# Output projection of a hybrid block: four of eight blocks of the contraction by seven half-size products

## The chip, the cores and the metric

The kernel runs on one core of a Trainium2 chip. A core has five engines that work side by side, each through its own instructions in order: TensorE (PE) multiplies matrices into PSUM, VectorE (DVE) and ScalarE (ACT) work elementwise, GpSimd (POOL) does small work and issues DMAs, and SyncE (SP) issues DMAs. They wait for each other on semaphores. The metric is the time of one execution on the device in microseconds (us); the times here are medians over several runs.

## The reference

One layer on x of 512 rows (tokens) by 1024 columns in fp32: a SwiGLU feed-forward half step, a mixer of dilated window attention and mLSTM, and a second feed-forward half step. What the change touches is the end of the mixer and the norm behind it:

```
merged = jax.nn.sigmoid(g_a) * (att @ w_att_branch) + jax.nn.sigmoid(g_m) * (ml @ w_mlstm_branch)
y = merged @ w_out                       # (512 x 1024) @ (1024 x 1024)
x = x + rmsnorm(y, mix_post_g)
f = swiglu(rmsnorm(x, ffn2_pre_g), ffn2_w_gate, ffn2_w_up, ffn2_w_down)
x = x + 0.5 * rmsnorm(f, ffn2_post_g)
```

All is computed to about fp32 precision. PE multiplies values of a shorter format (F32R), so that each operand is split in a high part, a rounded copy, and a low part, the rest, and each product is three: high by high, low by high, high by low.

## The kernel before

The kernel is one long program in stages: feed-forward 1, projections, attention, mLSTM, merge, output projection, feed-forward 2. It works on the 512 tokens as four tiles of 128 (index t), and keeps the activations of a product transposed, with the contracted dimension on the 128 partitions in 8 blocks (index dt or kk).

**Merge.** A loop over dt = 0 to 7 (`for dt in range(KD)`) makes block dt of the merged rows, transposed, 128 x 512: two products on PE, a few operations on DVE and ACT on `t1`, then ACT writes the high part meTh[:, dt] and DVE the low part meTl[:, dt]. The gates of block dt + 2 (tiles qa_gm, qb_gm) are computed in between.

**Output projection.** `down` goes over the eight blocks kk. `load_w` loads w_out's block of 128 x 1024 by a DMA from SP into a staging buffer wf (a ring of three), casts it on ACT to wh and computes the low part wl on DVE, five buffers each. `step` issues three 128x512 matmuls into one PSUM bank acc_o, for four token tiles and two column halves b: eight banks, all of PSUM. The first four blocks are multiplied block by block (kk < n - KEEP, with KEEP = 4). The last four are held and multiplied bank by bank, so that a token tile gets finished early.

**Norm behind it.** When tile t is complete, `PostNorm.bank` squares each bank on ACT (jk_pmx), sums on DVE (v_pmx), takes the power on POOL (r_pmx), and DVE multiplies by the gain (fg_mx) and adds to x. `prenorm` makes the next normed rows h_f of the tile in the same way (jk_f, v_f, r_f). Then PE transposes h_f into pt_f (`turn_norm`, eight transposes), ACT copies hTh_f from it and DVE computes hTl_f. The `todo` list issues these transposes between the matmuls of later banks, and the first products pg_b of feed-forward 2 read hTh_f and hTl_f by halves of 256 tokens. Their first weights, bgu00 and on, go through the same staging ring and `load_w`.

**Order.** The program is written once in Python; a planner then sets each engine's order by the costs and ready times that it assumes, keeping to the data's dependences. `Order` and `issue_after` pin a chain of instructions on an engine to the order in which they are written. The queues run strictly in that order on the chip.

The down products of both feed-forwards already work by seven products (class `Down`), and `down` already takes ready accumulators, with the second column half negated (flip).

Of the kernel before, what the change touches and what calls it, by code (L numbers as in the profile page):

```python
# [10 lines left out]
F32 = mybir.dt.float32  # L11
F32R = mybir.dt.float32r
BF16 = mybir.dt.bfloat16
AF = mybir.ActivationFunctionType
ALU = mybir.AluOpType

P = 128
T = 512
NT = T // P
D = 1024  # L20
KD = D // P
# [11 lines left out]
WMAX = 1024  # L33
# [6 lines left out]
def tile_hybrid_block(ctx: ExitStack, tc: tile.TileContext, a: dict):  # L40
    nc = tc.nc

    ids = ctx.enter_context(tc.tile_pool(name="ids", bufs=1))
    wpool = ctx.enter_context(tc.tile_pool(name="wpool", bufs=1))
    hpool = ctx.enter_context(tc.tile_pool(name="hpool", bufs=1))
    const = ctx.enter_context(tc.tile_pool(name="const", bufs=1, side="right"))
    act = ctx.enter_context(tc.tile_pool(name="act", bufs=1, side="right"))
# [10 lines left out]
    work = Work()  # L58
# [6 lines left out]
    def pair(name):  # L65
        return [bank(f"{name}_{b}") for b in range(2)]
# [22 lines left out]
    def load_w(src, name, n=1024, after=(), flip=False):  # L89
        wf = act.tile([P, WMAX], F32, tag="wf", bufs=3, name=f"wf_{name}")[:, :n]  # L90
        nc.sync.dma_start(wf, src)
        with ExitStack() as st:
            for i in after:
                st.enter_context(tc.issue_after(i))
            wh = wpool.tile([P, WMAX], F32R, tag="wh", bufs=5, name=f"wh_{name}")[:, :n]
            cast_w(wh, wf, flip)
            wl = wpool.tile([P, WMAX], F32R, tag="wl", bufs=5, name=f"wl_{name}")[:, :n]
            m = T if flip else n
            nc.vector.tensor_tensor(wl[:, :m], wf[:, :m], wh[:, :m].bitcast(F32), op=ALU.subtract)  # L99
            if flip:  # L100
                nc.vector.scalar_tensor_tensor(wl[:, T:], wf[:, T:], -1.0, wh[:, T:].bitcast(F32), op0=ALU.mult,
                                               op1=ALU.subtract)
        return wh, wl
# [146 lines left out]
    H = T // 2  # L250
    ADD, SUB, MUL = ALU.add, ALU.subtract, ALU.mult
# [410 lines left out]
    with new_pool("ffn_a") as fa:  # L662
# [99 lines left out]
        todo = []  # L762
# [596 lines left out]

    gctx = ExitStack()  # L1360
    mg = gctx.enter_context(tc.tile_pool(name="merge", bufs=1))
    meTh = mg.tile([P, KD, T], F32R, name="meTh")
    meTl = mg.tile([P, KD, T], F32R, name="meTl")
    class Tiles:
        def __init__(self, i):
            self.i = i
# [7 lines left out]
    for dt in range(KD):  # L1374
        if dt % 2 == 0:
            wA = load_w(a["wA"][dt // 2], f"wA{dt}")
        wM = load_w(a["wM"][dt], f"wM{dt}")
        p2 = pair(f"p2_{dt}")
        o = (dt % 2) * 512
        ws(p2[0], (wA[0][:, o:o + 512], wA[1][:, o:o + 512]), HEADS, atth, attl, (late, 6))  # L1380
        for _ in late:
            pass
        ws(p2[1], wM, KD, mlTh, mlTl)
        t1 = t1s[dt]
        for b in range(2):
            nc.vector.scalar_tensor_tensor(t1[:, b, :], t1[:, b, :], 1.0, p2[b], op0=ALU.add, op1=ALU.mult)
        nc.vector.tensor_tensor(t1[:, 0, :], t1[:, 0, :], t1[:, 1, :], op=ALU.add)
        nc.scalar.mul(meTh[:, dt, :], t1[:, 0, :], 0.5)
        nc.vector.scalar_tensor_tensor(meTl[:, dt, :], t1[:, 0, :], 0.5, meTh[:, dt, :].bitcast(F32),
                                       op0=ALU.mult, op1=ALU.subtract)  # L1390
        if dt + 2 < KD:
            late = branch_gates(dt + 2)
            next(late)
# [8 lines left out]
    def post2(t):  # L1402
        if t == 2:
            hT2.extend(new_hT("f2"))
        return PostNorm(t, g_mpost, [(work, "tmp"), (mm, "m0h")][t % 2], "mx")

    def finish2(t):
        h = prenorm(t, g_f2pre, [(work, "h"), (mm, "m0l")][t % 2], "f2")
        todo.append(lambda: turn_norm(t, h, *hT2, "f2"))

    pins = down(KD, lambda kk: a["wout"][kk], lambda kk: (meTh[:, kk, :], meTl[:, kk, :]), post2, finish2, todo, "o")
    gctx.close()
    mctx.close()

# [48 lines left out]
def _layout(inp):  # L1463
    f = lambda n: np.asarray(inp[n])[0]

    def cols(w):
        k, n = w.shape
        return w.reshape(k // P, P, n // P, P).transpose(2, 1, 0, 3).reshape(n // P, P, k)

    def rows(w):  # L1470
        k, n = w.shape
        return w.reshape(k // (2 * P), 2, P, n).transpose(0, 2, 1, 3).reshape(k // (2 * P), P, 2 * n)

    r = {"x": np.asarray(inp["x"])[0]}
    for i, n in ((1, "ffn1"), (2, "ffn2")):
        r[f"wgu{i}"] = np.concatenate([cols(f(f"{n}_w_gate")), cols(f(f"{n}_w_up"))], 2)
        wd = f(f"{n}_w_down").reshape(NF, P, D)
        r[f"wd{i}"] = wd
        wq = wd[:18].reshape(2, 9, P, 2, 512).transpose(0, 3, 2, 1, 4)
        r[f"wdq{i}"] = wq[:, :, :, :8].reshape(2, 2, P, 4, 1024).transpose(3, 0, 1, 2, 4)  # L1480
        r[f"wdh{i}"] = wq[:, :, :, 8]
        r[f"{n}_pre_g"], r[f"{n}_post_g"] = f(f"{n}_pre_g"), f(f"{n}_post_g")
    r["mix_pre_g"], r["mix_post_g"], r["mlstm_head_g"] = f("mix_pre_g"), f("mix_post_g"), f("mlstm_head_g")
    w = f("w_in")
    qa, ka, va = w[:, 0:1536], w[:, 1536:3072], w[:, 3072:4608]
    qkm, vm, om = w[:, 4608:6656], w[:, 6656:7680], w[:, 7680:8704]
    wi, wf_, ga, gm = w[:, 8704:8708], w[:, 8708:8712], w[:, 8712:9736], w[:, 9736:10760]
    place = np.arange(P)
    place[:64] = (place[:64] + 32) % 64

    def heads(w):
        w = w.reshape(D, 3, 4, P).copy()
        w[:, 1:] = w[:, 1:][..., place]
        return cols(w.reshape(D, 1536)).reshape(3, 4, P, D)

    q, k = heads(qa), heads(ka)
    r["wqk"] = np.stack([q, k], 2).transpose(1, 0, 2, 3, 4)
    v0g = [np.concatenate([va[:, h * 256:(h + 1) * 256], g], 1) for h, g in enumerate((wi, wf_))]
    r["wv0"] = np.stack([v.reshape(KD, P, 260).transpose(1, 0, 2).reshape(P, KD * 260) for v in v0g])

    v12 = [np.concatenate([va[:, 512 + h * P:512 + (h + 1) * P], va[:, 1024 + h * P:1024 + (h + 1) * P]], 1)
           for h in range(4)]
    r["wv12"] = np.stack([rows(np.concatenate(v12[2 * hp:2 * hp + 2], 1)) for hp in range(2)])
    r["gbias"] = np.stack([f("mlstm_i_bias"), f("mlstm_f_bias")], 1)
    qm, km = cols(qkm[:, 0:1024]), cols(qkm[:, 1024:2048])
    r["wmqk"] = np.stack([np.concatenate([qm[2 * h:2 * h + 2], km[2 * h:2 * h + 2]]) for h in range(4)])
    r["wvo"] = np.stack([rows(np.concatenate([vm[:, h * 256:(h + 1) * 256], om[:, h * 256:(h + 1) * 256]], 1))
                         for h in range(4)])
    r["wgm"] = np.stack([cols(ga), cols(gm)], 1)
    r["wA"] = cols(f("w_att_branch")).reshape(4, 2, P, 512).transpose(0, 2, 1, 3).reshape(4, P, 1024)  # L1510
    r["wM"] = cols(f("w_mlstm_branch"))
    r["wout"] = f("w_out").reshape(KD, P, D)
    cw = np.concatenate([f("conv_w"), f("conv_b")[None, :]], 0)
    r["convwb"] = cw.reshape(5, 16, P).transpose(2, 1, 0)
    return r
# [17 lines left out]
```

## Time and profile before

| What | Value |
|---|---|
| Median of 3 runs | 1333.09 us (1333.08 to 1333.26) |
| Profiled execution | 1333.12 us, its span 1331.2 us |
| Granted TensorE clock | 1.00 |
| PE busy | 1323.6 us, 99% |
| DVE, ACT, POOL busy | 1002.9, 640.4, 79.6 us |
| First and last matmul into acc_o start | 944.4 and 989.5 us |
| Matmuls into acc_o | 192, each 389 ns with overlap |

The page gives the busy time of each engine over the span. A matmul's busy time overlaps the next one's, so that the distance between two starts, not its length, says what it costs. "idle before" in brackets on a row is the time that an engine stood still, and the arrow names what ended it. The chain of waits goes back from the last instruction over whatever released each one. Times in windows and timelines are counted from the start of the span.

### The profile page before, as it was taken

What the parts mean: (1) busy time and instruction counts of PE and PEld (TensorE: products, weight loads), DVE (VectorE), ACT (ScalarE), POOL (GpSimd) and SP (SyncE); (2) the same over time, 40 slices, a digit from 0 to 9 for tenths busy, and PEclk for the clock granted to TensorE, in tenths of its full rate; (3) what the DMA queues carried; (4) which work ended last, traced back from release to release, by engine and by line L of the source; (5) the groups of instructions that cost most, each with busy time, mean ns of one, the idle gap of its engine ahead of it and who ended that gap; (6) DMA issues with size and microseconds to landing.
All of it is one profiled execution on the core that took longest, in us unless ns stands there. A gap on an engine that the chain in (4) does not pass through costs nothing.

```text
span 1331.2 us, 20808 instructions
## 1 busy us (share of the span) xinstructions
PE 1323.6 (99%) x8283; PEld 1197.0 (90%) x8283; DVE 1002.9 (75%) x1553; ACT 640.4 (48%) x1046; POOL 79.6 (6%) x118
## 2 busy tenths in 40 slices
PE   9999999999999999999999999999999999999998
PEld 9999999888998888888888889999889999999886
DVE  7999898798765556575756777776379999897886
ACT  6444444566634544544544444444265444445662
POOL 1000000230300000000000000000010000001220
PEclk9999999999999999999999999999999999999999
DMA  5333332896433422412222212335413333335972
GB/s 198 96 104 111 104 104 96 206 236 167 136 115 117 142 69 91 158 64 80 80 79 80 70 58 80 96 97 188 151 41 99 110 109 104 105 110 140 250 156 80
DMA packets 43906, 155.55 MB, mean 117 GB/s; under 512 B 4996, under 2 KB 5004, under 8 KB 43552
## 3 DMA queue, kind: packets, MB, share of 16 engines
q1 hardware_dynamic: 33120, 116.96, 26.6%
q0 software_dynamic: 10672, 37.25, 11.5%
q8 instruction: 65, 1.06, 0.3%
q14 instruction: 33, 0.27, 0.1%
q10 hardware_dynamic: 16, 0.00, 0.0%
HBM read 147.91 MB, written 6.29 MB: 116 GB/s over the span
## 4 chain that ended last, share of the span: by engine, by line
PE 99%; DVE 0%; DVEq 0%; POOLq 0%; ACT 0%; issue 0%; ACTq 0%
PE qb_b L338 10%; PE qb_a L338 10%; PE pq L189 8%; PE pm L189 7%; PE p L189 6%; PE qa_b L338 4%; PE qa_a L338 4%; PE qb_gm L1089 4%; PE acc_o L243 3%; PE accb_b L536 3%; PE accb_a L536 3%; PE pvo L1215 2%; PE pvo L1217 2%; PE pvo L1216 2%; PE accc_a L536 2%; PE accc_b L536 2%
## 5 line engine op out<-in xcount | busy, mean ns | idle before, releaser
L189 PE MATMUL pq<-hTh_mx,wh_qk 128*128 128x512 f32 x160 | 63.2, 395 | 0.0
L189 PE MATMUL pq<-hTl_mx,wh_qk 128*128 128x512 f32 x160 | 62.4, 390 | 0.0
L99 DVE TENSOR_TENSOR wl_qk<-wf_qk,wh_qk 128x1024 fp32r<-128x1024 f32 x24 | 29.4, 1223 | 31.1 <-ACT wh_qk L85 14.4
L189 PE MATMUL pm<-hTh_mx,wh_mqk 128*128 128x512 f32 x128 | 50.3, 393 | 0.0
L1215 PE MATMUL pvo<-wh_vo,hTh_mx 128*128 128x512 f32 x128 | 50.2, 392 | 0.0
L189 PE MATMUL pm<-hTl_mx,wh_mqk 128*128 128x512 f32 x128 | 49.9, 390 | 0.0
L1217 PE MATMUL pvo<-wl_vo,hTh_mx 128*128 128x512 f32 x128 | 49.9, 390 | 0.0
L1216 PE MATMUL pvo<-wh_vo,hTl_mx 128*128 128x512 f32 x128 | 49.8, 389 | 0.0
L99 DVE TENSOR_TENSOR wl_mqk<-wf_mqk,wh_mqk 128x1024 fp32r<-128x1024 f32 x16 | 19.6, 1224 | 35.7 <-ACT wh_mqk L85 26.7
L85 ACT CAST wh_qk<-wf_qk 128x1024 fp32r<-128x1024 f32 x24 | 25.0, 1046 | 40.6 <-issue 11.6
L189 PE MATMUL pq<-hTh_mx,wl_qk 128*128 128x512 f32 x160 | 39.6, 389 | 0.0
L263 ACT CAST wh_a<-cd_a 128x1024 fp32r<-128x1024 f32 x19 | 19.9, 1048 | 40.8 <-DVE cd_a L263 40.8
L263 ACT CAST wh_b<-cd_b 128x1024 fp32r<-128x1024 f32 x19 | 19.9, 1049 | 40.7 <-DVE cd_b L263 40.7
L338 PE MATMUL qa_b<-hTh_f,wh_b 128*128 128x256 f32 x152 | 38.2, 284 | 0.0
L338 PE MATMUL qa_a<-hTh_f,wh_a 128*128 128x256 f32 x152 | 38.2, 284 | 0.0
L338 PE MATMUL qa_b<-hTl_f,wh_b 128*128 128x256 f32 x152 | 38.1, 283 | 0.0
L338 PE MATMUL qa_a<-hTl_f,wh_a 128*128 128x256 f32 x152 | 38.1, 283 | 0.0
L85 ACT CAST wh_mqk<-wf_mqk 128x1024 fp32r<-128x1024 f32 x16 | 16.8, 1048 | 41.9 <-PE pvo L1216 22.9
L1010 DVE SCALAR_TENSOR_TENSOR z<-pm,cw,z 128x511 f32<-128x511 f32 (+2 forms) x48 | 35.3, 744 | 1.4 <-ACT z L1008 0.9
L189 PEld LDWEIGHTS pq<-hTh_mx,wl_qk 128*128 128x128 f32 x160 | 30.0, 188 | 6.2
L189 PEld LDWEIGHTS pq<-hTh_mx,wh_qk 128*128 128x128 f32 x160 | 30.1, 188 | 6.0
L189 PEld LDWEIGHTS pq<-hTl_mx,wh_qk 128*128 128x128 f32 x160 | 30.1, 188 | 6.0
(684 smaller groups left out, 4558.1 us busy)
## 6 DMA issues: line engine op xcount, KB each, us to landing
wf_qk<-in_wqk SPq DMA_DIRECT2D x24, 512.0 KB, 3.3
g_a<-in_wgu SPq DMA_DIRECT2D x19, 512.0 KB, 3.8
u_a<-in_wgu SPq DMA_DIRECT2D x19, 512.0 KB, 3.8
g_b<-in_wgu SPq DMA_DIRECT2D x19, 512.0 KB, 3.8
u_b<-in_wgu SPq DMA_DIRECT2D x19, 512.0 KB, 3.8
wf_mqk<-in_wmqk SPq DMA_DIRECT2D x16, 512.0 KB, 3.4
wf_vo<-in_wvo SPq DMA_DIRECT2D x16, 512.0 KB, 3.2
T_a<-in_wdq POOLq DMA_DIRECT2D x12, 512.0 KB, 10.9
```

The lines of the kernel that those rows point to most:

```text
L85: return nc.scalar.copy(wh, wf)
L99: nc.vector.tensor_tensor(wl[:, :m], wf[:, :m], wh[:, :m].bitcast(F32), op=ALU.subtract)
L189: nc.tensor.matmul(out, lhsT=wt[:, k * P:(k + 1) * P], rhs=x[:, k, 0:T], start=n == 0, stop=n == len(terms) - 1)
L243: nc.tensor.matmul(out, lhsT=x[:, tk], rhs=w[:, cs], start=first and n == 0, stop=last and n == 2, skip_group_check=True)
L263: self.last[eng] = getattr(getattr(nc, eng), fn)(*args, **kw).ins
L338: nc.tensor.matmul(out, lhsT=wt[:, i * P:(i + 1) * P], rhs=y[:, i, :], start=first and n == 0, stop=last and n == len(terms) - 1, skip_gro ...
L536: nc.tensor.matmul(o, lhsT=x[:, tk], rhs=w[:, cs], start=k in "1256" and g + m + n == 0, stop=False, skip_group_check=True)
L1010: nc.vector.scalar_tensor_tensor(z[:, s:], src[:, :T - s], cw[:, ct, 3 - s:4 - s], z[:, s:], op0=ALU.mult, op1=ALU.add)
L1089: nc.tensor.matmul(out, lhsT=wt[:, i * P:(i + 1) * P], rhs=y[:, i, :], start=first and m == 0, stop=last and m == len(terms) - 1, skip_gro ...
L1215: nc.tensor.matmul(out, lhsT=hTh[:, k, tk], rhs=wh[:, cs], start=k == 0, stop=False)
L1216: nc.tensor.matmul(out, lhsT=hTl[:, k, tk], rhs=wh[:, cs], start=False, stop=False)
L1217: nc.tensor.matmul(out, lhsT=hTh[:, k, tk], rhs=wl[:, cs], start=False, stop=k == KD - 1)
```

## The change

Blocks 0 to 3 of w_out (512 x 1024) and of the merged rows (512 tokens by 512) are no longer multiplied block by block. They form a product of 2 by 2 quadrants, with two token halves, two halves of the contraction and two column halves, which is computed by seven products of sums of quadrants. Each has two contraction blocks, two token tiles and one column half: 2 x 2 x 3 = 12 matmuls of 128x512.

- The merged rows of blocks 0 to 3 stay in fp32 (mef). Sums of them are built on DVE in S_o; each operand is cast to X_o on ACT and its low computed on DVE.
- The sums of weight quadrants are built by DMA: U0_o and U1_o are loaded and added to by accumulating DMAs from POOL during the merge (dt = 3), once more at the begin and once between products. Four quadrants also come raw through the staging ring as B_o, by SP.
- The results meet in PSUM: four copies on ACT to S_o and in-place additions on DVE (`middle`).
- Blocks 4 to 7 are held as before. Column half b = 1 is now negated, so that the cast and the low of each held weight come in two halves, and PostNorm uses the negated form for b = 1.

```diff
--- before.py
+++ after.py
@@ -1359,8 +1359,133 @@
 
     gctx = ExitStack()
     mg = gctx.enter_context(tc.tile_pool(name="merge", bufs=1))
-    meTh = mg.tile([P, KD, T], F32R, name="meTh")
-    meTl = mg.tile([P, KD, T], F32R, name="meTl")
+    mef = mg.tile([P, 4, T], F32, name="mef")
+    meTh = mg.tile([P, KD - 4, T], F32R, name="meTh")
+    meTl = mg.tile([P, KD - 4, T], F32R, name="meTl")
+
+    class Out7:
+        steps = "2165734"
+
+        def __init__(self):
+            self.do, self.x, self.w = Order(), {}, {}
+            self.added, self.lowered = 0, 0
+            self.U = [mg.tile([P, 2, T], F32, name=f"U{i}_o") for i in range(2)]
+            self.B = {}
+            for i in range(2):
+                self.get("gpsimd", self.U[i], (0, 0))
+                self.get("gpsimd", self.U[i], (0, 1), accum_op=ADD)
+            self.get("gpsimd", self.U[1], (1, 1), accum_op=ADD)
+
+        def get(self, eng, t, k, **kw):
+            self.do(eng, "dma_start", t, halves(a["woq"][k], T), **kw)
+
+        def begin(self):
+            self.X = hpool.tile([P, KD, T], F32R, tag="hTh", name="X_o")
+            self.S = hpool.tile([P, KD, T], F32, tag="hTl", name="S_o")
+            for k in ((1, 0), (0, 0), (0, 1)):
+                self.raw(k)
+            self.get("gpsimd", self.B[0, 1], (1, 1), accum_op=ADD)
+
+        def raw(self, k):
+            self.B[k] = act.tile([P, 2, T], F32, tag="wf", bufs=3, name=f"B{k[0]}{k[1]}_o")
+            self.get("sync", self.B[k], k)
+
+        def tt(self, out, p, q, op=ADD):
+            self.do("vector", "tensor_tensor", out, p, q, op=op)
+
+        def stt(self, out, p, q):
+            self.do("vector", "scalar_tensor_tensor", out, p, -1.0, q, op0=MUL, op1=SUB)
+
+        def slot(self, i):
+            return halves(self.S[:, i, :], H)
+
+        def sums(self, s):
+            A = lambda i, k: mef[:, 2 * k:2 * k + 2, i * H:(i + 1) * H]
+            B, U, S = self.B, self.U, self.slot
+            if s == "2":
+                src = A(0, 1), B[1, 0]
+            elif s == "1":
+                src = A(0, 0), B[0, 0]
+            elif s == "6":
+                self.tt(S(0), A(1, 1), A(1, 0), SUB)
+                self.stt(S(1), S(0), A(0, 0))
+                src = S(1), U[1]
+            elif s == "5":
+                src = S(0), U[0]
+            elif s == "7":
+                self.tt(S(2), A(0, 0), A(1, 0), SUB)
+                src = S(2), B[0, 1]
+            elif s == "3":
+                self.stt(S(1), A(0, 1), S(1))
+                src = S(1), B[1, 1]
+            else:
+                src = A(1, 1), U[1]
+            return src
+
+        def front(self, n):
+            while self.added <= min(n, 6):
+                i, s = self.added, self.steps[self.added]
+                x, w = self.sums(s)
+                wh, wl = (wpool.tile([P, WMAX], F32R, tag=f"w{y}", bufs=5, name=f"w{y}{s}_o") for y in "hl")
+                xh, xl = (self.X[:, 2 * (i % 4) + j, :] for j in range(2))
+                self.w[s] = w, halves(wh, T), halves(wl, T)
+                self.x[s] = x, halves(xh, H), halves(xl, H)
+                for v, h, _ in (self.w[s], self.x[s]):
+                    self.do("scalar", "copy", h, v)
+                self.added += 1
+
+        def back(self, n):
+            while self.lowered <= min(n, 6):
+                s = self.steps[self.lowered]
+                for v, h, l in (self.w[s], self.x[s]):
+                    self.tt(l, v, h.bitcast(F32), SUB)
+                if s == "2":
+                    self.raw((1, 1))
+                elif s == "6":
+                    self.get("gpsimd", self.U[1], (1, 0), accum_op=ADD)
+                self.lowered += 1
+
+        def product(self, s):
+            (_, wh, wl), (_, xh, xl) = self.w[s], self.x[s]
+            for n, (x, w) in enumerate(((xh, wh), (xh, wl), (xl, wh))):
+                for m in range(2):
+                    for i, o in enumerate(self.out[s]):
+                        nc.tensor.matmul(o, lhsT=x[:, m, i * P:(i + 1) * P], rhs=w[:, m, :],
+                                         start=s in "1256" and m + n == 0, stop=False, skip_group_check=True)
+
+        def middle(self, s):
+            S, (a_, b_, c_, d_) = self.S, (self.out[k] for k in "2651")
+            v = [S[:, 3, :], S[:, 0, :]]
+            for i in range(2):
+                if s in "15":
+                    self.do("scalar", "copy", S[:, (4 if s == "1" else 6) + i, :], self.out[s][i])
+                elif s == "6":
+                    self.tt(v[i], b_[i], S[:, 4 + i, :])
+                elif s == "7":
+                    self.tt(d_[i], b_[i], S[:, 6 + i, :])
+                elif s == "3":
+                    self.tt(c_[i], c_[i], v[i])
+                elif s == "4":
+                    self.tt(b_[i], b_[i], S[:, 4 + i, :])
+                if s == "3":
+                    self.tt(a_[i], a_[i], S[:, 4 + i, :])
+            if s == "5":
+                self.tt(S[:, 6:8, :], S[:, 6:8, :], S[:, 4:6, :])
+
+        def run(self):
+            self.accs = [[None, None] for _ in range(NT)]
+            where = {}
+            for n, ts, b in (("2", (0, 1), 0), ("1", (2, 3), 1), ("6", (2, 3), 0), ("5", (0, 1), 1)):
+                where[n] = [bank(f"acc_o{t}{b}") for t in ts]
+                for t, o in zip(ts, where[n]):
+                    self.accs[t][b] = o
+            self.out = {**where, "3": where["5"], "7": where["6"], "4": where["6"]}
+            for n, s in enumerate(self.steps):
+                self.front(n + 3)
+                self.back(n + 2 if n != 4 else 5)
+                self.product(s)
+                self.middle(s)
+
     class Tiles:
         def __init__(self, i):
             self.i = i
@@ -1375,6 +1500,12 @@
         if dt % 2 == 0:
             wA = load_w(a["wA"][dt // 2], f"wA{dt}")
         wM = load_w(a["wM"][dt], f"wM{dt}")
+        if dt == 3:
+            out7 = Out7()
+        if dt == KD - 1:
+            out7.begin()
+            out7.front(2)
+            out7.back(2)
         p2 = pair(f"p2_{dt}")
         o = (dt % 2) * 512
         ws(p2[0], (wA[0][:, o:o + 512], wA[1][:, o:o + 512]), HEADS, atth, attl, (late, 6))
@@ -1385,9 +1516,12 @@
         for b in range(2):
             nc.vector.scalar_tensor_tensor(t1[:, b, :], t1[:, b, :], 1.0, p2[b], op0=ALU.add, op1=ALU.mult)
         nc.vector.tensor_tensor(t1[:, 0, :], t1[:, 0, :], t1[:, 1, :], op=ALU.add)
-        nc.scalar.mul(meTh[:, dt, :], t1[:, 0, :], 0.5)
-        nc.vector.scalar_tensor_tensor(meTl[:, dt, :], t1[:, 0, :], 0.5, meTh[:, dt, :].bitcast(F32),
-                                       op0=ALU.mult, op1=ALU.subtract)
+        if dt < 4:
+            nc.scalar.mul(mef[:, dt, :], t1[:, 0, :], 0.5)
+        else:
+            nc.scalar.mul(meTh[:, dt - 4, :], t1[:, 0, :], 0.5)
+            nc.vector.scalar_tensor_tensor(meTl[:, dt - 4, :], t1[:, 0, :], 0.5, meTh[:, dt - 4, :].bitcast(F32),
+                                           op0=ALU.mult, op1=ALU.subtract)
         if dt + 2 < KD:
             late = branch_gates(dt + 2)
             next(late)
@@ -1402,13 +1536,15 @@
     def post2(t):
         if t == 2:
             hT2.extend(new_hT("f2"))
-        return PostNorm(t, g_mpost, [(work, "tmp"), (mm, "m0h")][t % 2], "mx")
+        return PostNorm(t, g_mpost, [(work, "tmp"), (mm, "m0h")][t % 2], "mx", flip=True)
 
     def finish2(t):
         h = prenorm(t, g_f2pre, [(work, "h"), (mm, "m0l")][t % 2], "f2")
         todo.append(lambda: turn_norm(t, h, *hT2, "f2"))
 
-    pins = down(KD, lambda kk: a["wout"][kk], lambda kk: (meTh[:, kk, :], meTl[:, kk, :]), post2, finish2, todo, "o")
+    out7.run()
+    pins = down(KD, lambda kk: a["wout"][kk], lambda kk: (meTh[:, kk - 4, :], meTl[:, kk - 4, :]), post2, finish2, todo,
+                "o", out7.accs, 4)
     gctx.close()
     mctx.close()
 
@@ -1510,6 +1646,7 @@
     r["wA"] = cols(f("w_att_branch")).reshape(4, 2, P, 512).transpose(0, 2, 1, 3).reshape(4, P, 1024)
     r["wM"] = cols(f("w_mlstm_branch"))
     r["wout"] = f("w_out").reshape(KD, P, D)
+    r["woq"] = r["wout"][:4].reshape(2, 2, P, 2, 512).transpose(0, 3, 2, 1, 4).reshape(2, 2, P, 1024)
     cw = np.concatenate([f("conv_w"), f("conv_b")[None, :]], 0)
     r["convwb"] = cw.reshape(5, 16, P).transpose(2, 1, 0)
     return r
```

Three places show how the instructions move. On SP, at the end of the merge, the eight loads of w_out's blocks (wf_od) stood behind the last merge weights. Before:

```order
L91 DMA wf_wM_9065<-in_wM 128x1024
L91 DMA wf_od_9134<-in_wout 128x1024
L91 DMA wf_od_9164<-in_wout 128x1024
L91 DMA wf_od_9194<-in_wout 128x1024
L91 DMA wf_od_9224<-in_wout 128x1024
L91 DMA wf_od_9254<-in_wout 128x1024
```

and with the change four raw quadrants B_o, then the blocks 4, 5, 6, 7, then feed-forward 2's first weights:

```order
L91 DMA wf_wM_9069<-in_wM 128x1024
L263 DMA B_o<-in_woq 128x1024 x4
L91 DMA wf_od_9295<-in_wout 128x1024
L91 DMA wf_od_9303<-in_wout 128x1024
L91 DMA wf_od_9311<-in_wout 128x1024
L91 DMA wf_od_9319<-in_wout 128x1024
L91 DMA wf_bgu_9580<-in_wgu 128x1024
L91 DMA wf_bgu_9586<-in_wgu 128x1024
```

The number of loads through the ring is the same; the third load behind wf_od_9295 (block 4) reuses its buffer, and that is wf_od_9319 (block 7).

On DVE, at the end of the seven products. The number behind acc_o is a bank's, wl4_o is the low of the last product's weight, and od4 to od7 are the held blocks. With the change:

```order
L263 TENSOR_TENSOR wl4_o_9229<-U1_o_8478,wh4_o_9228 128x1024
L263 TENSOR_TENSOR X_o_9075<-mef_7982,X_o_9075 128x512
L263 TENSOR_TENSOR acc_o01_9168<-acc_o01_9168,S_o_9076 128x512
L263 TENSOR_TENSOR acc_o00_9162<-acc_o00_9162,S_o_9076 128x512
L263 TENSOR_TENSOR acc_o11_9169<-acc_o11_9169,S_o_9076 128x512
L263 TENSOR_TENSOR acc_o10_9163<-acc_o10_9163,S_o_9076 128x512
L263 TENSOR_TENSOR acc_o20_9166<-acc_o20_9166,S_o_9076 128x512
L263 TENSOR_TENSOR acc_o30_9167<-acc_o30_9167,S_o_9076 128x512
L99 TENSOR_TENSOR wl_od4_9300<-wf_od4_9295,wh_od4_9297 128x512
L101 SCALAR_TENSOR_TENSOR wl_od4_9300<-wf_od4_9295,wh_od4_9297 128x512
```

Before, the lows of the held blocks stood among the last merge operations:

```order
L1386 SCALAR_TENSOR_TENSOR t1_7_8891<-t1_7_8891,p2_7_1_9072 128x512
L99 TENSOR_TENSOR wl_od4_9258<-wf_od4_9254,wh_od4_9256 128x1024
L1387 TENSOR_TENSOR t1_7_8891<-t1_7_8891 128x512
L1389 SCALAR_TENSOR_TENSOR meTl_7983<-t1_7_8891,meTh_7982 128x512
L99 TENSOR_TENSOR wl_od5_9264<-wf_od5_9260,wh_od5_9262 128x1024
L99 TENSOR_TENSOR wl_od6_9270<-wf_od6_9266,wh_od6_9268 128x1024
L99 TENSOR_TENSOR wl_od7_9276<-wf_od7_9272,wh_od7_9274 128x1024
L99 TENSOR_TENSOR wl_bgu00_9535<-wf_bgu00_9531,wh_bgu00_9533 128x1024
```

So the low of block 4 has moved behind all additions into PSUM.

On PE, around the transposes of tile 1 (pt_f21), in the held blocks. With the change they stand behind the first two matmuls of bank acc_o31, the last bank, with ten to go:

```order
L243 MATMUL acc_o30_9167<-wl_od7_9324,meTh_7983 128x512
L243 MATMUL acc_o31_9165<-wh_od4_9297,meTh_7983 128x512
L243 MATMUL acc_o31_9165<-wh_od4_9297,meTl_7984 128x512
L155 MATMUL pt_f21_0_9513<-ident_79,h_f21_9417 128x128 x4
L155 MATMUL pt_f21_1_9514<-ident_79,h_f21_9417 128x128 x4
L243 MATMUL acc_o31_9165<-wl_od4_9300,meTh_7983 128x512
```

Before, the transposes of tile 0 and of tile 1 each stood ahead of the twelve held matmuls of a bank of tile 3, b = 0 and b = 1; now some matmuls with od4's weights are brought forward, ahead of od7's first use, which is the 31st matmul of the 96 held ones.

## The prediction

> **What bounds the kernel now.** I read the page first, then the waits of PE, the chain of waits around the output projection, the busy time by stage, and the timelines of DVE, ACT and SP there.
>
> ```profile
> span 1331.2 us, 20808 instructions
> PE 1323.6 (99%) x8283; PEld 1197.0 (90%) x8283; DVE 1002.9 (75%) x1553; ACT 640.4 (48%) x1046; POOL 79.6 (6%) x118
> ...
> PE 99%; DVE 0%; DVEq 0%; POOLq 0%; ACT 0%; issue 0%; ACTq 0%
> ```
>
> ```profile
> PE warm L74 <- DVE nhalf L81: 1.1, 1, 1.1
> PE g_f1pre L690 <- DVE gcol L263: 0.3, 1, 0.3
> ```
>
> PE is the bound, and these two rows are all that its waits hold in the whole program, both in the opening. So a matmul less is time won, if no wait comes up behind it. The chain through the projection:
>
> ```profile
> 944.57 38.08 PE acc_o L243 x168
> 982.65 0.87 PE pt_f L155 x8
> 983.52 2.75 PE acc_o L243 x12
> 986.28 0.87 PE pt_f L155 x8
> 987.15 2.74 PE acc_o L243 x12
> ```
>
> The 192 matmuls of the projection run back to back, 38.08 / 168 = 0.2267 us each, split only by the transposes pt_f of the next stage's input. The stage by engine (busy us and count of PE, PEld, DVE, ACT, POOL, the granted clock, DMA share, GB/s):
>
> ```profile
> 944.40:966.20 21.80, 21.80 (x98) 18.05 (x97) 6.80 (x7) 3.79 (x5) 0.00 (x0) 1.00 0.31 97
> 966.20:989.90 23.70, 23.70 (x115) 19.81 (x114) 16.94 (x32) 13.32 (x34) 3.32 (x6) 1.00 0.08 23
> ```
>
> DVE and ACT idle for two thirds of the first half, and in the second they carry the norm of four 128-row tiles, whose result PE transposes. Its chain, on DVE:
>
> ```profile
> 967.26 1.23 DVE L99 TENSOR_TENSOR wl_bgu<-wf_bgu,wh_bgu 128x1024 fp32r<-128x1024 f32 x1 [4.21 <-ACT wh_bgu L85]
> ...
> 972.59 0.16 DVE L125 SCALAR_TENSOR_TENSOR v_pmx<-sp_mx 128x1 f32<-128x1 f32 x1 [2.09 <-ACT jk_pmx L121]
> ...
> 978.25 0.16 DVE L125 SCALAR_TENSOR_TENSOR v_pmx<-sp_mx 128x1 f32<-128x1 f32 x1 [0.24 <-ACT jk_pmx L121]
> ...
> 982.56 0.49 DVE L146 TENSOR_SCALAR h_f<-h_f,r_f 128x512 f32<-128x512 f32 x1 [0.73 <-POOL r_f L114]
> ...
> 983.88 0.16 DVE L125 SCALAR_TENSOR_TENSOR v_pmx<-sp_mx 128x1 f32<-128x1 f32 x1 [0.24 <-ACT jk_pmx L121]
> 984.56 1.28 DVE L159 TENSOR_TENSOR hTl_f<-pt_f,hTh_f 128x512 fp32r<-128x512 f32 x2
> ```
>
> From v_pmx to the next v_pmx it takes 5.66 and 5.63 us a tile, while PE gives a tile 24 matmuls, 5.44 us. So the norm is no faster than PE, and it keeps up by its head start: h_f of tile 1 is ready at 982.56 + 0.49 = 983.05, and its transposes begin at 986.28, a reserve of 3.2 us. That reserve is what the change spends.
>
> **The change part by part.** *PE.* Blocks 0 to 3 took 4 x 8 x 3 = 96 matmuls, now seven products of 12, 84. Twelve go: 12 x 0.2267 = **-2.72 us**. I take the same interval for the new ones, since such products exist further on:
>
> ```profile
> 1239.96 10.20 PE accc_b L536 x45
> 1250.16 12.01 PE accb_b L536 x53
> ```
>
> 10.20 / 45 and 12.01 / 53 are 0.2267 again. In this trace's time the products run from 944.40 to 944.40 + 84 x 0.2267 = 963.44.
>
> *DVE, ACT in the merge.* Four lows meTl go (0.69 each, DVE); sums, lows of seven weights and seven operands come. A weight costs what wl_od costs (1.23 on DVE, 1.05 on ACT), an operand half of it. They are spread from 928 to 962, and the window above has DVE busy 6.80 of 21.80. I set the rows' durations one behind the other in each engine's printed order, with each wait for the row that releases it, and found no wait of PE inside the products: 0 us. The tightest is the low of the last weight, wl4: DVE ends it at 960.4 behind two additions, and PE uses it at its fifth matmul of product 4, 944.40 + 76 x 0.2267 = 961.6. Anything that makes DVE over 1.2 us late there is a wait of PE for the excess.
>
> *POOL.* Seven accumulating or first loads of weights. Five are issued right after r_m, in a gap of 109 us:
>
> ```profile
> 920.84 1.11 POOL L1397 DMA_DIRECT2D x<-xkeep  x2 [109.38 <-PE qb_gm L1089]
> ```
>
> The other two: the sum for product 7 is issued at about 932 and first used by PE at 944.40 + 4 x 2.72 = 955.3; the last addition for product 4, at about 938, is used at 960.7, and ACT comes to its cast at 952.4. Adding loads elsewhere in the trace (min, median, max of one tile's):
>
> ```profile
> DMA to landing us min/median/max: 3.6/10.0/16.9
> ```
>
> Bounds: at 10.0 both land before ACT asks (948 against 952.4), 0 us; at 16.9 the cast comes 2.8 us late, and with it all that is queued behind it on ACT, the copies for DVE's additions too: with the 1.2 us in hand PE waits 1.6, and at most the whole 2.8. After 940 only single loads are in flight, so I take 0.
>
> *The load that turns late.* This carries the prediction. The three staging buffers first hold four raw blocks, so wf_od7 gets its buffer only when wl_od4 is computed, and wl_od4 stands on DVE behind the six last additions into PSUM. Durations:
>
> ```profile
> 1262.59 1.29 DVE L263 TENSOR_TENSOR accc_b<-accb_b,S_b 128x512 f32<-128x512 f32 x2
> ...
> 915.69 1.61 SPq L91 DMA_DIRECT2D wf_wM<-in_wM  x2
> ...
> wf_wM<-in_wM SPq DMA_DIRECT2D x1, 512.0 KB, 3.3
> wf_wM<-in_wM SPq DMA_DIRECT2D x1, 512.0 KB, 4.2
> ```
>
> Two additions take 1.29, so 0.60 from start to start. The last two wait for product 4: 963.4, 964.0; the two halves of wl_od4 end at 965.9; SP issues the load then; 3.3 us later, 969.2, it lands; ACT casts the halves by 969.9 and 970.4 and DVE ends the lows at 970.6 and 971.2. PE wants wh_od7 at its 31st matmul of the held blocks, 963.44 + 30 x 0.2267 = 970.24, the second half at 970.7, the lows at 970.9 and 971.6. Just in time, by 0.3 us: 0, and each 0.3 us more of landing is up to 0.3 of wait.
>
> *What is late next.* wf_bgu00 follows in the same ring, when wl_od5 is done, 1.2 us after wf_od7. The pair of loads above was issued 1.61 - 0.33 = 1.28 us apart and landed 1.28 + 4.2 - 3.3 = 2.2 apart. So bgu00 lands at 969.2 + 2.2 = 971.4; alone it would take:
>
> ```profile
> wf_bgu<-in_wgu SPq DMA_DIRECT2D x1, 512.0 KB, 3.8
> ```
>
> thus 967.15 + 3.8 = 970.9. The Trainium skill ("DMA: Bandwidth & Descriptors", Bandwidth) puts the ceiling at 435 GB/s; 512 KB are 1.2 us by it, an estimate, and bgu00 would not be held up. The pair's 2.2 us are 240 GB/s; by the page the sum would be the -0.8 below, and I go by the pair.
>
> On ACT the cast of bgu00 stands ahead of the squares of tile 0, and on DVE its low ahead of fg_mx:
>
> ```profile
> 966.18 1.05 ACT L85 CAST wh_bgu<-wf_bgu 128x1024 fp32r<-128x1024 f32 x1 [4.39 <-PE acc_o L243]
> 969.08 0.60 ACT L121 ACTIVATE jk_pmx<-acc_o 128x512 bf16<-128x512 f32 x1 [1.85 <-PE acc_o L243]
> 969.58 0.20 ACT L121 ACTIVATION_READ_ACCUMULATOR jk_pmx<-acc_o 128x1 f32 x1
> ...
> 969.80 0.69 DVE L176 TENSOR_TENSOR fg_mx<-acc_o,g_mpost 128x512 f32<-128x512 f32 x1 [1.31 <-ACT jk_pmx L121]
> ```
>
> Before, cast and low were over by 968.5, before the squares. Now the cast runs 971.5 to 972.6, the low to 973.8, fg_mx to 974.4, and v_pmx of tile 0 stands at **974.3** instead of 972.59. From there to h_f of tile 1 it was 983.05 - 972.59 = 10.46 us; now the two hTl_f copies of tile 0's transposes (1.28 together, above) stand ahead of it, of which one, 0.6, falls on the path: 974.3 + 10.5 + 0.6 = 985.4. PE comes to these transposes, which now stand ten matmuls further forward, at 963.44 + 86 x 0.2267 + 0.87 = 983.81. **+1.6 us** of wait (+1.1 with bgu00 landing at 970.9).
>
> Behind that PE stays just ahead of the chain: the matmul pg_b on hTl_f of tile 1 waits **+0.4** (its low stands behind the norm of tile 2 on DVE), the transposes of tile 3 **+0.5**. These two come from the same arithmetic; what bounds them is 0, if the first wait already brings PE behind the chain, and 2 x (5.65 - 5.44) + 0.6 = 1.0, if it stays at the chain's pace. The same arithmetic over the order of before gives 983.0 for h_f of tile 1, where the trace has 983.05, and no wait.
>
> Sum: -2.72 + 1.6 + 0.4 + 0.5 = **-0.2 us** on the paired load, -2.72 + 1.1 + 0.9 = -0.7 (with every row set behind its releaser, -0.8) on a lone one. The profiled execution took 1333.12 us, 1.9 around its span of 1331.2 and 0.03 above the median of the runs, 1333.09. I predict 1333.1 - 0.3 = **1332.8 us**. The seven-product saving is real on PE and nearly all of it becomes wait.
>
> **Rivals.** *The whole saving* (1333.1 - 2.7 = 1330.4): h_f of tile 1 would have to be ready at 983.8, so v_pmx at 972.7. For it: block acc_o00 itself is complete at 963.44 + 34 x 0.2267 = 971.2, and without the cast the squares could end by 972.8. Against it: the order on ACT and DVE puts bgu00's cast and low first. 0.05.
>
> *Slower, by a late wf_od7*: one load in the merge, issued beside POOL's loads, took
>
> ```profile
> wf_od<-in_wout SPq DMA_DIRECT2D x1, 512.0 KB, 6.2
> ```
>
> At 6.2 instead of 3.3, PE waits 2.6 at its 31st held matmul, and bgu00 and the whole norm chain move with it, so the waits behind stay: -2.72 + 2.6 + 2.5 = +2.4, 1335.5. It decides from a landing above 3.7 on, where the sum turns positive. For it: everything hangs on one load with 0.3 us to spare. Against it: POOL's loads are over by 950, and near 966 the DMA share is 0.08 in the window above. 0.10, of which 0.07 over the bound below.
>
> *Slower, by an adding load at 16.9 us*: up to +2.8 on top of -0.2, 1335.7. 0.04, half of it over the bound.
>
> *Not what it says* — products slower than 0.2267 each, by a bank that is written every other matmul: the rows of accc_b show the same pattern at full rate. 0.01.
>
> That leaves **0.80** for the forecast. Its own range is 1332.2 to 1333.5: 0.8 down with a lone landing, and up by 0.3 to 0.6 with landings later by as much. The range for 8 in 10 reaches somewhat to both rivals: 1331.4 to 1334.2. A measurement here tells about 0.2%, 2.7 us, from no change: faster by more needs the whole saving, 0.05; slower by more 0.09; within it 0.86.
>
> **What would show it.** Right: 12 matmuls fewer on PE; waits of PE on h_f of tile 1 of 1 to 2 us, then on hTl_f and h_f of tile 3, about 2 to 2.5 together; wf_od7 issued about 22 us after the first product and used at once; v_pmx of tile 0 some 30 us after the first product instead of 28.2. Wrong: a wait of PE inside the products (operands late); a wait on wh_od7 of over a microsecond; no wait at pt_f (the chain is not late); or a span shorter by 2.7.

## The result, and the profile after

The change makes the kernel slower: 1335.35 us (median of 20 runs, 1334.71 to 1336.32) against 1333.22 us (1333.00 to 1333.52), a ratio of 1.0016 with a 95% interval of 1.0010 to 1.0022. The forecast was 1332.8 with a range that ended at 1334.2.

The head of the profile's page after, and the waits of PE:

```profile
span 1333.2 us, 20847 instructions
PE 1322.2 (99%) x8271; PEld 1194.6 (90%) x8271; DVE 1017.4 (76%) x1578; ACT 649.4 (49%) x1064; POOL 85.1 (6%) x125
```

```profile
PE pt_f L155 <- DVE h_f L146: 2.7, 3, 1.9
PE warm L74 <- DVE nhalf L81: 1.1, 1, 1.1
PE g_f1pre L690 <- DVE gcol L263: 0.3, 1, 0.3
```

PE has twelve matmuls less, 8283 to 8271, and it has new waits, all of them in this view for h_f at the transposes pt_f. The products themselves run without one (the tile view of X_o; columns: duration in ns as min/median/max, first and last start):

```profile
L1453 PE MATMUL acc_o<-wh_o,X_o x56: 389/389/389, 944.6 to 963.4; 128*128 128x512 f32 x56
```

The profiled span is 2.0 us longer than before, 1333.2 against 1331.2. Three marks divide it. The first matmul of the stage starts at 944.56 instead of 944.40, 0.16 later; this comes from the stretch ahead of the stage, and since the other profiles of this study lie there between 0.1 earlier and 0.4 later than that of before, I count it as chance. The first product of feed-forward 2's seven-product loop, qa_b, in the chain of waits after, is here:

```profile
1016.09 10.91 PE pg_b L189 x48
1027.00 1.43 PE qa_b L338 x12
```

Before, that row read

```profile
1025.57 1.43 PE qa_b L338 x12
```

so PE is 1.43 us late there, 1.27 of which arose between the projection and this point: 2.72 saved and 4.0 lost. The last matmuls keep that distance (1.46). The other 0.5 us lie behind the last matmul, in a drain of POOL's queue at the end of the program. The view of that source line, after and before, counts three drains (min/median/max in ns, first and last start in us); the long one starts first, and only two of 0.1 us and less follow it:

```profile
L1666 POOLq DRAIN  x3: 51/98/4871, 1327.5 to 1332.9; - x3
```

```profile
L1529 POOLq DRAIN  x3: 51/98/4339, 1326.1 to 1330.9; - x3
```

It takes 4.87 us instead of 4.34. 0.16 + 1.27 + 0.03 + 0.53 is the whole difference of 2.0.

Where the 4.0 us come from is seen on ACT and DVE after (timelines, with the idle time before a row and its releaser in brackets):

```profile
969.74 0.62 ACT L86 CAST wh_od<-wf_od 128x512 fp32r<-128x512 f32 x1 [10.07 <-DMA wf_od<-in_wout]
970.26 0.63 ACT L87 ACTIVATE wh_od<-wf_od 128x512 fp32r<-128x512 f32 x1
972.83 1.05 ACT L85 CAST wh_bgu<-wf_bgu 128x1024 fp32r<-128x1024 f32 x1 [1.94 <-DMA wf_bgu<-in_wgu]
973.78 0.59 ACT L121 ACTIVATE jk_pmx<-acc_o 128x512 bf16<-128x512 f32 x1
```

```profile
973.91 1.23 DVE L99 TENSOR_TENSOR wl_bgu<-wf_bgu,wh_bgu 128x1024 fp32r<-128x1024 f32 x1 [2.23 <-ACT wh_bgu L85]
975.05 0.69 DVE L176 TENSOR_TENSOR fg_mx<-acc_o,g_mpost 128x512 f32<-128x512 f32 x1
975.65 0.15 DVE L125 SCALAR_TENSOR_TENSOR v_pmx<-sp_mx 128x1 f32<-128x1 f32 x1
```

ACT stands still for 1.94 us until bgu00 has landed, casts it, and only then squares tile 0, whose first bank was complete some two microseconds earlier (where the cast is out of the way, in cast_behind below, PE releases this square at 971.56). v_pmx of tile 0 stands at 975.65, 3.1 us later than before. The issues on SP, and two of their landings (the DMA view of a window that holds one issue; the last column is us from issue to landing):

```profile
966.13 0.33 SPq L91 DMA_DIRECT2D wf_od<-in_wout  x1
967.30 4.74 SPq L91 DMA_DIRECT2D wf_bgu<-in_wgu  x3
...
wf_od<-in_wout SPq DMA_DIRECT2D x1, 512.0 KB, 3.5
wf_bgu<-in_wgu SPq DMA_DIRECT2D x1, 512.0 KB, 5.4
```

wf_od7 took 3.5 us, bgu00 5.4. At the transposes of tile 1, PE then stood for 1.93 us:

```profile
984.44 0.39 PE L243 MATMUL acc_o<-wh_od,meTl 128*128 128x512 f32 x1
986.76 0.98 PE L155 MATMUL pt_f<-ident,h_f 128*128 128x128 f32 x7 [1.93 <-DVE h_f L146]
```

From start to start it lost 2.1 there (986.76 - 984.44 - 0.23), 0.4 at the transposes of tile 0, 0.3 at hTl_f of tile 1 and 0.75 at the transposes of tile 3, 0.2 on wf_od7. That is 3.7 of the 4.0; the last 0.3 is in small steps that I did not follow. The waits at tile 0 and on wf_od7 were not in the forecast.

### The profile page after: what moved, and what is told of

Its sections match the earlier page's. It is cut to its first block, busy times and chain, and to the rows that moved or that the text cites. A ratio compares the mean times of both kernels' runs of the same rounds, so it can differ in the third digit from the quotient of the medians.

```text
span 1333.2 us, 20847 instructions
## 1 busy us (share of the span) xinstructions
PE 1322.2 (99%) x8271; PEld 1194.6 (90%) x8271; DVE 1017.4 (76%) x1578; ACT 649.4 (49%) x1064; POOL 85.1 (6%) x125
```

## The experiments

Theory: three loads are in flight at once (wf_od7, bgu00 and, 1.2 us behind it, bgu01), which share the DMA engines; bgu00, in the middle, lands later than a pair of loads would let it; and since its cast heads the queue of ACT, the norm of tile 0 and with it all tiles are late. Rivals: bgu00's load is slow by itself; the transposes stand too early; the loss is in the products. For the drain: it grows with the number of DMAs that POOL issued.

The medians below are of 10 or 11 runs each (turn_late of 5), and the kernel before ran beside them on the same chip: 1333.25 us in the first group of four, 1333.12 in the second, 1333.10 in the third. The change itself stands at 1335.35, from its own 20 runs. A profile shows one execution: that of the change took 1335.01 us, that of skip_buf 1333.58, its fastest, and the others lie within 0.4 of their medians.

**One load held back (skip_buf).** A ring buffer is taken by a tile with one written column until the norm of tile 0 has begun, so bgu01 waits for the next buffer.

```diff
+        if name == "bgu01":
+            skip = act.tile([P, WMAX], F32, tag="wf", bufs=3, name="wf_skip")
+            ...  # issued after square and x of tile 0
+            nc.vector.memset(skip[:, 0:1], 0.0)
```

> The change, with one staging buffer held back, so that the load of bgu01 cannot be issued behind wf_od7 and bgu00 (968.5 us) but only when wl_od7 is done (about 971.5); nothing else is moved. Theory (crowding: three loads of 512 KB in flight share the DMA engines, and bgu00, the middle one, lands 5.4 us after its issue instead of the 4.2 of the second load of a pair): bgu00 lands in 4.3 us or less, at 971.6; the norm of tile 0 (v_pmx) moves from 975.65 to about 974.5; the waits of PE shrink by about 1.1 us; time about 1334.2 us, 1.1 under the change. Rival (a load of w_gate/w_up behind another is slow by itself, or what counts is the place of the transposes): bgu00 still lands in about 5.4 us, or the wait at the transposes of tile 1 stays 1.9 us; time 1335.3.

Measured: 1334.32 us (1333.58 to 1334.69), 1.03 under the change. bgu00's row, and v_pmx of tile 0:

```profile
wf_bgu<-in_wgu SPq DMA_DIRECT2D x1, 512.0 KB, 4.2
...
974.22 0.15 DVE L135 SCALAR_TENSOR_TENSOR v_pmx<-sp_mx 128x1 f32<-128x1 f32 x1
```

```profile
PE pt_f L165 <- DVE h_f L156: 1.9, 2, 1.3
```

Of the loads up to bgu00 none was moved, only the one behind it, and bgu00 landed in 4.2 us instead of 5.4. The landing, v_pmx and the time come within 0.3 us of what the theory expected; a load that takes 5.4 us by itself is out.

**The cast behind the norm (cast_behind).**

```diff
-                           after=pins if f < EARLY and f + b else ()) for b in range(2)]
+                           after=(pins if f + b else norm0) if f < EARLY else ()) for b in range(2)]
```

norm0 holds the second square and the new x of tile 0.

> The change, with the cast of bgu00 on ACT ordered behind the squares of tile 0, and its low on DVE behind x of tile 0; loads as in the change. Theory (late norm: the cast that waits for a late load stands ahead of the norm of tile 0): the squares start at about 971.5 instead of 973.8, v_pmx of tile 0 at 973 instead of 975.65, whenever bgu00 lands; the wait at the transposes of tile 1 falls from 1.9 us to 0.3 or less, all waits of PE behind the products from 4.0 to about 1.8 (hTl_f of tile 1 and the transposes of tile 3 remain, since the low of 1.2 us now stands inside the chain); time about 1333.2, 2.1 under the change. Rival (the transposes simply stand too early): the wait at tile 1 stays over 1 us, time 1334.5 or more.

Measured: 1333.64 us (1333.40 to 1333.92), 1.71 under the change. The load of bgu00 was as late as in the change, and the norm did not mind:

```profile
wf_bgu<-in_wgu SPq DMA_DIRECT2D x1, 512.0 KB, 5.5
...
973.04 0.16 DVE L129 SCALAR_TENSOR_TENSOR v_pmx<-sp_mx 128x1 f32<-128x1 f32 x1
```

```profile
PE pt_f L159 <- DVE h_f L150: 1.2, 2, 0.6
...
PE pg_b L209 <- DVE hTl_f L163: 0.6, 1, 0.6
```

The wait at tile 1 fell from 1.9 to 0.6, not to 0.3 as expected, and the gain is 1.7 instead of 2.1: the low of bgu00, 1.2 us on DVE, now stands inside the norm's chain and makes tile 1 later. It does so by way of POOL, whose power r_f of tile 0 takes 1.41 us beside this low, where it took 0.56 in the change:

```profile
976.56 1.22 DVE L101 TENSOR_TENSOR wl_bgu<-wf_bgu,wh_bgu 128x1024 fp32r<-128x1024 f32 x1
```

```profile
976.78 1.41 POOL L116 TENSOR_TENSOR r_f<-v_f,nhalf 128x1 f32<-128x1 f32 x1 [2.87 <-DVE v_f L129]
```

DVE's part of h_f of tile 0 then ends 2.22 us behind the start of v_f, against 1.38 in the change. The spread of the runs also shrank, from 1.6 us in 20 runs to 0.5 in 11, as it should if what varied from run to run was the landing of one load; that it was is not shown.

**A buffer for block 4 (od4_own).** U0_o's memory is free once product 5's weight is lowered.

```diff
+    own["od4"] = out7.U[0].rearrange("p a b -> p (a b)")
     out7.run()
...
+        wf = own.pop(name, None)
+        if wf is None:
+            wf = act.tile([P, WMAX], F32, tag="wf", bufs=3, name=f"wf_{name}")[:, :n]
```

> The change, with block 4 of w_out loaded into the memory of U0_o, which is free after product 5's weight is lowered, instead of the staging ring: the ring moves up by one, and wf_od7 is issued at about 955 instead of 966. The planner puts the low of bgu00 behind the first power of the norm. Theory (crowding and late norm): v_pmx of tile 0 at about 971.5 instead of 975.65, no wait at the transposes of tiles 0 and 1; PE instead waits about 2 us at the first products pg_b, whose weight casts and hTh_f now come last on ACT; time about 1333.4. Rival (bgu00 is not what is late): waits at the transposes stay, time 1335.3.

Measured: 1333.76 us (1333.62 to 1334.19). v_pmx of tile 0 at 971.41, no wait at pt_f of the second norm. The waits went to the first products, where bgu01's cast is late:

```profile
PE pg_b L207 <- ACT wh_bgu L85: 1.4, 1, 1.4
...
PE pg_b L207 <- ACT hTh_f L162: 0.6, 2, 0.4
```

**Both out of the ring (both_own).** As od4_own, and bgu00 is loaded into U1_o's memory.

```diff
+    own["bgu00"] = out7.U[1].rearrange("p a b -> p (a b)")
+    first2 = [load_w(a["wgu2"][0, :, b * 1024:(b + 1) * 1024], f"bgu0{b}", after=pins if b else ()) for b in range(2)]
```

> The change, with block 4 of w_out loaded into the memory of U0_o and bgu00 into that of U1_o, so that neither goes through the staging ring: wf_od7 is issued at about 955, bgu00 at about 960.5, and no late load stands ahead of the norm. Theory (late norm): v_pmx of tile 0 at 971.4 instead of 975.65, no wait of PE at the transposes; what is left of the 4.0 us are waits at the first products pg_b for hTh_f of tile 1 and for the cast of bgu01, 0.6 and 0.8, with what surrounds them about 2 in all; POOL's drain stays 4.87; time about 1333.0, 2.3 under the change. Rival (more is lost in the seven products themselves or in their additions): over 1334.

Measured: 1332.44 us (1332.18 to 1333.17), 2.9 under the change and 0.7 under the kernel before (ratio 0.9995). The interval, 0.9986 to 1.0003, includes 1, though all but one of the 11 runs lie under every run of the kernel before. ACT casts bgu00 before the held blocks have delivered tile 0 and then waits for PE, as it did before the change:

```profile
964.46 1.05 ACT L85 CAST wh_bgu<-U_o 128x1024 fp32r<-128x1024 f32 x1 [2.16 <-DMA U_o<-in_wgu]
969.99 0.60 ACT L125 ACTIVATE jk_pmx<-acc_o 128x512 bf16<-128x512 f32 x1 [4.48 <-PE acc_o L247]
```

```profile
PE pg_b L207 <- ACT wh_bgu L85: 0.8, 1, 0.8
```

```profile
1024.54 1.43 PE qa_b L342 x12
```

qa_b begins 1.03 us earlier than before instead of 1.43 later, although this execution also began 0.22 late. One wait of 0.8 is left at bgu01. So the seven products do save time on PE once the norm starts on time, 1.25 us of the 2.72. The expectation was 1333.0; of the waits for hTh_f that it named next to none came (0.1), which goes the way of the difference.

**The transposes later (turn_late).**

```diff
-                if (t, b) in ((2, 1), (3, 0)):
+                if (t, b) in ((2, 1), (3, 1 if name == "o" else 0)):
```

> The change, with the transposes of tile 1 issued behind all matmuls of the last bank, ten matmuls (2.3 us) later; nothing else in the norm is moved. Theory (the norm is late, wherever the transposes stand): the wait at the transposes of tile 1 goes, and comes back, larger, at the first products pg_b, which need hTh_f and hTl_f of tile 1: about 4 us there, time 1336.5 to 1337.5. Rival (the transposes were put too early, and the wait is only theirs): 1.9 us of wait go, time about 1333.4.

Measured: 1338.15 us (1337.72 to 1340.18), 2.8 over the change.

```profile
PE pg_b L203 <- ACT hTh_f L158: 3.8, 2, 3.3
```

The wait moved to the first products and grew, as the theory has it, to 3.8 us where about 4 were expected; the time is 0.65 over the expected range, and I did not follow where that comes from. That the transposes stand too early is out.

One measure takes these five runs together, the time on PE from the first matmul into acc_o to the first into qa_b: 81.00 us before, 82.27 with the change, 80.99 in skip_buf and in cast_behind, 81.13 in od4_own, 79.75 in both_own, 85.68 in turn_late.

**The drain.** drain14 and drain7 add 14 and 7 DMAs of 4 KB from POOL to the kernel before, into memory that nobody reads; drain_less moves ten from POOL to SP, drain_m4 four, drain_m8 eight. The core of the first, and of drain_m4:

```diff
+            for i in range(14):
+                nc.gpsimd.dma_start(junk14[:, i, :], a["wout"][0][:, 8 * i:8 * i + 8])
```

```diff
-        nc.gpsimd.dma_start(xs[t], xkeep[t])
+        nc.sync.dma_start(xs[t], xkeep[t])
```

> The kernel before, with 14 more DMAs from POOL of 4 KB each, early in the merge, into memory that nobody reads. In the change the last instruction of POOL's queue (a drain at the program's end) took 4.87 us instead of 4.34, and 0.5 us of its longer span lie there; it has 7 more DMAs from POOL. Theory (the drain grows with the number of DMAs that POOL issued, 0.076 us each): the drain takes 5.4 us, the time is 1.06 us longer, 1334.2. Rival (it goes by bytes or by chance): drain 4.3, time 1333.2.

> The kernel before, with ten DMAs moved from POOL's queue to SP's (four stores and four loads of xkeep, two gains); nothing else. Theory (the drain at the end grows by 0.06 to 0.076 us for each DMA that POOL issued): drain 3.6 to 3.75 us instead of 4.34, time 1332.5 to 1332.65. Rival (it depends on bytes late in the program, or on chance): 1333.25.

> The kernel before with 7 more DMAs from POOL, as many as the change adds, but of 4 KB instead of 512 KB, early in the merge, into memory that nobody reads. So far the drain took 4.14, 4.34, 4.87 and 5.19 us with 75, 80, 87 and 94 DMAs from POOL, but 6.38 with 70. Theory (above 70 the count sets it): 4.87 us, the drain of the change, with a time of 1333.6. Rival (the bytes or the adding kind set it): about 4.4 us, time 1333.2.

> The kernel before with the four loads of x out of xkeep on SP's queue instead of POOL's: 76 DMAs from POOL. If the count alone sets the drain, it lies between those of 75 and 80, 4.14 and 4.34 us, and the time at about 1333.0. If moving these loads is what made it 6.38 us with 70, it is again over 6 us, time about 1335.

> The kernel before with the four stores and the four loads of xkeep on SP's queue: 72 DMAs from POOL. If the drain is a curve with a jump somewhere between 70 and 75, this is either about 4.0 us (time 1332.8) or about 6.4 (time 1335.1), and tells on which side of the jump 72 lies; if it is a straight line from 6.38 at 70 down to 4.14 at 75, about 5.5 us.

The drain's row in drain_m8 and in drain7:

```profile
L1529 POOLq DRAIN  x3: 51/98/6544, 1326.0 to 1333.1; - x3
```

```profile
L1533 POOLq DRAIN  x3: 51/98/4788, 1326.1 to 1331.4; - x3
```

| Kernel | DMAs from POOL | Drain, us | Median, us |
|---|---|---|---|
| drain_less | 70 | 6.38 | 1335.09 |
| drain_m8 | 72 | 6.54 | 1335.50 |
| best_e (below) | 75 | 4.14 | 1332.14 |
| drain_m4 | 76 | 4.09 | 1333.65 |
| before | 80 | 4.34 | 1333.10 to 1333.25 |
| drain7 | 87 | 4.79 | 1333.63 |
| the change and its variants with 87 | 87 | 4.87 | |
| drain14 | 94 | 5.20 | 1334.05 |

drain7 answers the question about the change: seven more DMAs of 4 KB, with nothing of the change in it, lengthen the drain by 0.45 us and the time by 0.53. So from 80 to 87 the number is enough, without the bytes or the adding. My expectation for drain_less was wrong, and not in size: with ten DMAs fewer the drain is 2 us longer. The values lie on two rising pieces, 0.05 to 0.08 us for each DMA (but for 75 and 76, which are 0.04 apart the other way), with a fall of some 2.4 us between 72 and 75. What happens there in the hardware or its software the runs don't show, nor whether the number alone makes the fall: 70 and 72 were reached by moving the stores and loads of xkeep in the kernel before, and the 75 of best_e, which moves them too, by way of another kernel. drain_m4 is slower than before by 0.55 although its drain is 0.25 shorter. Its rows at the end of the program show another engine:

```profile
L1529 POOLq DRAIN  x3: 51/93/4094, 1326.7 to 1331.8; - x3
L1529 SPq DRAIN  x3: 7/7/23, 1331.2 to 1331.7; - x3
```

POOL's drain was over at 1326.65 + 4.09 = 1330.7, and SP came to its own drain only at 1331.2; the engines end together after the later of the two. In the kernel before they were 0.1 apart, POOL last (1330.4, SP 1330.3). Of the 0.9 by which SP is later, 0.3 is there already at the last matmul, 0.3 more comes from POOL's last power r_pf, which starts later behind v_pf, and the rest, 0.3, lies between the landing of the last store and SP's drain: 0.42 us here and 0.15 before. That last stretch is 0.14 to 0.15 in every profile with 230 DMAs on SP and 0.39 to 0.47 in the three with 234, 238 and 242 that record the landing. So SP's end is later by some 0.3 where it has more DMAs, and that is as much as this profile shows of it; why r_pf started late, and how much of the 0.55 of the medians is SP's, stays open, since no run measured SP's share by itself.

**Both, and fewer DMAs on POOL (best_e).** both_own, and twelve DMAs on SP instead of POOL: the first copies of U0_o and U1_o, the stores and loads of xkeep, two gains.

> As both_own, and twelve DMAs go from POOL's queue to SP's: the first copies of U0_o and U1_o, the four stores of x and the four loads of it (xkeep), the gains mpost and f2pre; 75 DMAs from POOL are left of 87. Theory: drain at the end 4.87 - 12 x 0.06 to 0.076 = 4.0 to 4.15 us, the rest as both_own, time about 1332.2, faster than the kernel before by about 1 us. Rival (SP's queue delays weight loads behind these, or the drain does not depend on the count): 1333.0 or more.

Measured: 1332.14 us (1331.73 to 1332.67) against 1333.12 (1332.90 to 1333.50), a ratio of 0.9992 with an interval of 0.9983 to 1.0001, which just includes 1; yet no run of the one reaches a run of the other. The drain took 4.14 us. Against both_own it is 0.30 better, though the drain is 0.73 shorter. Here too SP's end comes behind POOL's long drain:

```profile
L1673 POOLq DRAIN  x3: 51/93/4135, 1324.9 to 1329.9; - x3
...
L1673 SPq DRAIN  x3: 7/7/7, 1329.4 to 1329.7; - x3
```

POOL's drain is over at 1324.9 + 4.1 = 1329.0 and SP's begins at 1329.4, which takes 0.4 of the 0.73 back.

## Why the prediction was wrong

The forecast put the saving on PE at 2.72 us and let 2.5 of it turn into waits of PE behind the norm. The mechanism was right: bgu00's late cast holds the norm, and PE waits at the tiles that were named, 2.1, 0.3 and 0.75 us where 1.6, 0.4 and 0.5 were forecast. Two terms of the sum were not right, the landing of bgu00, which was put too early, and the end of the program, which was left out. (The step from the sum of -0.2 to the -0.3 that was taken off the median has no row behind it.)

- **12 x 0.2267 = -2.72, products at full rate, no wait inside them:** right. They run from 944.56 to 963.6 with 389 ns each, and no wait falls among them.
- **The adding loads of POOL at 0 us:** right. The six loads into U_o, two first copies and four additions, landed in 3.6 to 7.6 us, far from the 16.9 of the upper bound.
- **wf_od7 just in time:** right to 0.2 us. It landed 3.5 us after its issue (3.3 forecast), and PE lost 0.2 us on it where 0 was forecast. The rival that named a time near the measured one, 1335.5, did so by a wf_od7 that lands in 6.2 us; that did not happen.
- **"So bgu00 lands at 969.2 + 2.2 = 971.4":** this step failed, in its size. It took a pair of loads as the model, and there were three: bgu01 was issued 1.2 us behind bgu00, at 968.50, into the buffer of block 6. bgu00 landed at 967.30 + 5.4 = 972.7, 1.3 later than forecast (0.9 of it is the distance to the landing of wf_od7, 3.1 instead of 2.2; 0.2 is wf_od7's own landing, and 0.16 the later start of the stage), and v_pmx came at 975.65 instead of 974.3, by the same 1.3. skip_buf shows that the third load is the cause: without it bgu00 lands in 4.2 us, the paired value, and the time falls by 1.03. The waits of 2.5 us became 4.0, with 0.4 at the transposes of tile 0 and 0.3 of small steps that no term named. The same rows decide against the estimate from the ceiling of 435 GB/s in the Trainium skill ("DMA: Bandwidth & Descriptors", Bandwidth), by which bgu00 would not have been held up: it was, by two neighbours, though the ceiling was not reached. From 966 to 976 us the DMA engines moved a mean of 211 GB/s, and at most 393 in any of the forty slices of the view (the DMA view of this stretch):

```profile
DMA packets 577, 2.11 MB, mean 211 GB/s; under 512 B 64, under 2 KB 64, under 8 KB 576
```

- **The sum itself left out a term:** the end of the program. Seven more DMAs from POOL were costed where they are issued, at nothing, and not where POOL's queue is drained. That term is 0.53 us by the change's profile, and drain7's time grew by as much.

-0.2 + 1.5 + 0.53 gives +1.8; with the 0.16 ahead of the stage it is the profiled +2.0, and the medians differ by 2.1. The first of the two terms is shown by skip_buf, cast_behind and both_own, the second by drain7. The range was too narrow because both bounds of the landing came from rows with at most two loads in flight.

## What to carry to other kernels

When a change leaves the same number of loads in a staging ring but lets several buffers come free in one burst, cost the landing of each from rows with that many loads in flight, and look at what stands behind its cast in the engine's queue: an early-written cast that waits for a load can hold a chain that needs nothing of it. Memory that an earlier step has just given up, here the weight sums, is a staging buffer for what comes next. And count the DMAs that a change adds to POOL's queue also at the program's end.

## What the runs showed of the hardware

- Loads of 512 KB from SP, issued 1.2 us apart, in the profiles of this stage: the first lands in 3.3 to 3.9 us, the second in 4.2 when it is the last (skip_buf) and in 5.4 to 5.9 when a third follows (the change, cast_behind, turn_late, both_own, best_e). A later load delays an earlier one.
- The power of a norm on POOL, on 128 x 1 values, takes 0.54 to 0.72 us in 376 records of these profiles, and 1.41 to 1.47 in the other 40, all of them beside a weight's low (128 x 1024) on DVE; why is not shown.
- The drain of POOL's queue at the end of the program takes 4.1 to 6.5 us. It goes with the number of DMAs that POOL issued anywhere in the program, some 0.05 to 0.08 us more for each, but 2.4 us less from 72 to 75; that the number alone sets it is shown from 80 to 94. It lies on the path that sets the end as long as SP's own end is earlier, and moving DMAs off POOL made the program slower in three of four cases.
